# A hybrid encoder on one core: smaller first pieces, a 32-column level, narrow idle products

## The chip, the cores and the metric

The kernel runs on one core of one Trainium2 chip. The metric is the device time of one execution in microseconds. TensorE (PE) multiplies matrices, VectorE (DVE), ScalarE (ACT) and GpSimd (POOL) do the elementwise work, and SyncE (SP) issues most DMA transfers. Every engine works through its own instructions in order.

## The reference, cut to what matters

The input is `x`, 256 tokens by 2048 features, in float32. Two layers follow, and a final RMSNorm. Each layer is RMSNorm, a token mixer, a residual add, RMSNorm, a gated MLP with a depthwise convolution of width 3 (ConvGLU, 5504 hidden features), and a residual add. The mixer of the first layer is a bidirectional mLSTM (8 heads), that of the second a bidirectional HGRN2 (16 heads of 128).

```python
for layer in range(DEPTH):
    hn = rmsnorm(h, norm_mix_g[layer])
    mix = mlstm_mixer(hn, ...) if layer % 2 == 0 else hgrn_mixer(hn, ...)
    h = h + mix
    h = h + conv_glu(rmsnorm(h, norm_ffn_g[layer]), ...)
return rmsnorm(h, final_g)

# HGRN2, one direction: a product of gates f lies between a token t and a source s
lf = log(lb + (1 - lb) * sigmoid(z));  k = (1 - lb) * sigmoid(-z)
attn[t, s] = sum_k q[t, k] * exp(sum of lf over (s, t]) * k[s, k]      # s <= t
o[t] = sum_s attn[t, s] * v[s]                                         # and the same backward in time
```

## The kernel before, in words

**Products and weights.** All weights are read once from memory in float32. ACT rounds each piece to a high part `wh` (line 152), DVE subtracts it from the piece to get the low part `wl` (line 153), and TensorE forms high by high, high by low and low by high. The activations are split in the same way into `xt`: the high half by ACT (line 224), the low half by DVE (line 225). A stream of chunks goes through `stream`, which asks `split_weights` for pieces, three ahead. A piece is loaded by SP into one of three buffers `raw` (line 138, `RAW = 3`); it can be loaded only when DVE has done the last `wl` of the piece that had the buffer. There are four buffers each of `wh` and `wl` (`WB = 4`).

**The first chunk.** It has 16 k-tiles. One k-tile is 128 features: 640 columns of weights (512 for the values of the first heads and 128 for the gates) and 256 columns of `x`. `FIRST` lists the k-tiles at which a piece begins. The x tiles lie in `gx`; tiles 0 and 1 are loaded on ACT's queue (line 143), the later ones by SP, right behind the weights of their piece (line 146). For every k-tile, ACT makes `wh`, DVE makes `wl`, and then `ch.x` splits the x tile; `pin` keeps these in the order in which the program states them. TensorE then makes eight products a tile (lines 213 to 218). At k-tile 10, SP also loads two tables of constants, `cst` and `pp` (line 240). Elsewhere a scheduler orders the instructions of each engine by its own estimate of times, so that an edit in one place can move instructions in another. The chunk after the first is `in_w_aq`, with pieces of 2048 columns (1 MB).

**Idle products.** Before the first chunk TensorE multiplies a tile of ones by itself nine times (line 875). Nothing reads the result. A float32 product is two passes in the records, so this shows as 18.

**HGRN2 heads.** The second layer forms `attn` by levels. At the level of h tokens, pairs of neighbouring blocks of h tokens are joined, for h = 1, 2, 4, ... 64, and 128 by two full products (lines 735 and 736). The operands of levels 1 to 64 are kept as `ms[0]` to `ms[6]`. `product` (line 711) makes eight products, one for each block of 32 source tokens, each of them 32 output partitions high; four neighbours write the four quarters of the partitions. In `pa` (PSUM, 512 columns) lie the full products, level 64 (`ms[6]`) and level 32 (`ms[5]`), both with 64 columns for each block; in `pd` lie the five levels 1 to 16 and the diagonal (`ks`, `q`), with 32 columns for each block. For level 32 the columns are both blocks of the pair, although only the neighbour's block is needed; the other half is overwritten later. ACT copies the diagonal to `AD` (line 742), DVE selects each of the five levels into it under a mask (line 744), ACT copies `pa` to `AT` (line 745) and then puts the four diagonal blocks of `AD` into `AT` (line 748). TensorE multiplies `AT` by the values (`py`, line 759). The generator `head` is advanced by `side.tick` while TensorE runs the chunks, and yields between these stages.

Of the kernel before, what the change touches and what calls it, by code (L numbers as in the profile page):

```python
# [15 lines left out]
P = 128  # L16
T = 256
# [26 lines left out]
WB = 4  # L44
MIX = 5
LEAD = 48
FIRST = (0, 1, 2, 4, 7, 10, 13, 16)

QUAD = 32
LEVELS = (1, 2, 4, 8, 16, 32, 64)  # L50
# [5 lines left out]
def trunk_kernel(ctx, tc, xT, x_d, fg_d, pp_d, cst_d, w_first, w_aq, w_ak, w_av, w_ao, w_aout,  # L56
                 w_bq, w_bv, w_bg, w_bout, w_up, w_down, out, mscr):
    nc = tc.nc
    act, dve, pool, pe = nc.scalar, nc.vector, nc.gpsimd, nc.tensor
# [9 lines left out]
    ones = keep.tile([P, T], F32, name="ones")  # L69
# [12 lines left out]
    def aux(name):  # L82
        return psa.tile([P, 512], F32, tag="aux", name=name)
# [39 lines left out]
    def split_weights(chunks):  # L123

        first = True
        for ch in chunks:
            total = ch.nk * ch.width
            cuts = [0]
            if first:
                cuts = [k * ch.width for k in FIRST]  # L130
            while cuts[-1] < total:
                cuts.append(min(total, cuts[-1] + 2048))
            step = ch.width if first else 1024
            for b0, b1 in zip(cuts, cuts[1:]):
                n = b1 - b0
                raw = wpool.tile([P, 2048], F32, tag="raw", bufs=RAW, name="raw")
                pin = tc.keep_in_program_order if first else lambda ins: ins
                pin(nc.sync.dma_start(raw[:, :n], ch.src[:, b0:b0 + n]))
                if first:
                    k0, k1 = b0 // ch.width, b1 // ch.width  # L140
                    if k0 == 0:
                        for a, b in ((0, KT + T), (KT + T, KT + 2 * T)):
                            nc.scalar.dma_start(gx[:, a:b], xT[:, a:b])
                    elif k0 > 1:
                        a, b = KT + k0 * T, KT + k1 * T
                        pin(nc.sync.dma_start(gx[:, a:b], xT[:, a:b]))
                for c0 in range(0, n, step):
                    m = min(step, n - c0)
                    wh = wpool.tile([P, 1024], F32R, tag="wh", bufs=WB, name="wh")
                    wl = wpool.tile([P, 1024], F32R, tag="wl", bufs=WB, name="wl")  # L150
                    r = raw[:, c0:c0 + m]
                    pin(act.copy(wh[:, :m], r))  # L152
                    pin(dve.tensor_tensor(wl[:, :m], r, wh[:, :m].bitcast(F32), ALU.subtract))  # L153
                    if first:
                        ch.x((b0 + c0) // ch.width, pin)
                    yield wh, wl, m // ch.width
            first = False

    def stream(chunks):
        pieces = split_weights(chunks)  # L160
        ready = []

# [213 lines left out]
    def head_scale(ss, width):  # L376
        rs = ev.tile([P, 2], F32, tag="rs", bufs=6, name="rs")
        dve.tensor_scalar(rs, ss, 1.0 / width, EPS, ALU.mult, ALU.add)
        pool.tensor_tensor(rs, rs, hmx, ALU.pow)
        return rs  # L380
# [242 lines left out]
    def hgrn(norm, nxt):  # L623
# [25 lines left out]
        def blocks(z, h, a, b):  # L649
            v = z[:, 0:2 * (T + h)].rearrange("k (p x) -> k p x", p=2)[:, :, a:b]  # L650
            return v.rearrange("k p (m j) -> k m p j", j=2 * h)[:, :, :, 0:h]

        def gview(g, n, start, h):
            v = g[:, start:start + 2 * (n - 1)].rearrange("k (p x) -> k p x", p=2)[:, :, 0::2]
            return v.rearrange("k p m -> k m p").unsqueeze(3).broadcast_to([P, n // 2, 2, h])
# [28 lines left out]
        def head(hd):  # L684
            mp = box["mp"]
            st = heads[hd]
            while hd and "done" not in heads[hd - 1]:
                yield 0.3
            QZ, KZ = st["QK"][:, 0:640], st["QK"][:, 512:1152]
            q, ks, G = st["q"], st["ks"], st["G"]  # L690
            AT = mp.tile([P, 4, P], F32, tag="AT", bufs=2, name="AT")
            AD = mp.tile([P, 2, QUAD], F32, tag="AD", bufs=2, name="AD")

            def gather(h):

                i = box["turn"] % (4 + MIX)
                box["turn"] += 1
                if i < 4:
                    m = keep.tile([P, 2, T], F32, tag=f"yt{KT - 4 + i}", name=f"kq{i}")
                else:  # L700
                    m = mp.tile([P, 2, T], F32, tag="kq", bufs=MIX, name="kq")
                for j, z in enumerate((KZ, QZ)):
                    dve.tensor_copy(m[:, j].rearrange("k (m p j) -> k m p j", p=2, j=h), blocks(z, h, 0, T))  # L703
                return m[:, 0], m[:, 1]

            def product(pd, k, q, n, at):

                for b in range(8):
                    o, c, t = b % 4 * QUAD, b // 4 * pd.shape[1] // 2, at(b)
                    c += t % P if pd.shape[1] == T else 0  # L710
                    pe.matmul(pd[o:o + QUAD, c:c + n], k[:, b * QUAD:(b + 1) * QUAD], q[:, t:t + n], start=True, stop=True)  # L711

            def both(ps):
                return ps.rearrange("p (a b) -> p a b", a=2)

            step = SPREAD if hd < BH - 2 else STEP
            mask = [cst[:, C_LV + i * QUAD:C_LV + (i + 1) * QUAD].bitcast(I32).unsqueeze(1).broadcast_to([P, 2, QUAD])
                    for i in range(FINE)]
            ms, n = [gather(1)], T
            yield step  # L720
            for li, h in enumerate(LEVELS):
                qa, ka = blocks(QZ, h, 0, T), blocks(KZ, h, 0, T)
                dve.tensor_tensor(ka, ka, gview(G, n, 1, h), ALU.mult)
                dve.tensor_tensor(qa, qa, gview(G, n, n + 1, h), ALU.mult)
                if h < 64:
                    ms.append(gather(2 * h))
                    n //= 2
                    G2 = mp.tile([P, 3 * n], F32, tag=f"G{h}", bufs=2, name="G2")
                    pool.tensor_tensor(G2, G[:, 0:6 * n:2], G[:, 1:6 * n:2], ALU.mult)  # L729
                    G = G2  # L730
                else:
                    st["done"] = True
                yield step
            pa, pd = aux("pa"), aux("pd")
            pe.matmul(pa[:, 2 * P:3 * P], KZ[:, 0:P], QZ[:, T + P:2 * T], start=True, stop=True)
            pe.matmul(pa[:, 3 * P:4 * P], KZ[:, T + P:2 * T], QZ[:, 0:P], start=True, stop=True)  # L736
            product(pa[:, 0:T], *ms[6], 64, lambda b: (b // 2 ^ 1) * 64)
            product(pa[:, 0:T], *ms[5], 64, lambda b: b // 2 * 64)
            for i in reversed(range(FINE)):
                product(pd[:, (i + 1) * 64:(i + 2) * 64], *ms[i], QUAD, lambda b: b * QUAD)  # L740
            product(pd[:, 0:64], ks, q, QUAD, lambda b: b * QUAD)
            act.copy(AD, both(pd[:, 0:64]))
            for i in range(FINE):
                dve.copy_predicated(AD, mask[i], both(pd[:, (i + 1) * 64:(i + 2) * 64]))
            act.copy(AT, pa.rearrange("p (a b) -> p a b", a=4))
            for j in range(4):
                o = slice(j * QUAD, (j + 1) * QUAD)
                act.copy(AT[o, 0:2, o], AD[o])
            yield
            while "V" not in st["qd"]:  # L750
                yield
            V, j = st["qd"]["V"], hd % 4
            py = aux("py")
            y = mp.tile([P, T], F32, tag="y", bufs=4, name="y")
            ss = mp.tile([P, 2], F32, tag="ss", bufs=2, name="ss")
            for t in range(2):
                c = slice(t * P, (t + 1) * P)
                for s in range(2):
                    pe.matmul(py[:, c], AT[:, s if s == t else 2 + s], V[:, s, j * P:(j + 1) * P], start=(s == 0), stop=(s == 1))  # L759
            act.copy(y, py[:, 0:T])  # L760
            for t in range(2):
                jk = ev.tile([P, 512], F32, tag="jk", bufs=1, name="jk")
                act.activation(jk[:, 0:P], y[:, t * P:(t + 1) * P], AF.Square, accum_out=ss[:, t:t + 1])
            st["y"] = (y, head_scale(ss, 128))
# [106 lines left out]
    pool.memset(pad, 0.0)  # L871
    pool.memset(pad[:, 0:4:2], 1.0)
    idle = aux("idle")
    for _ in range(9):
        pe.matmul(idle[:, 0:P], ones[:, 0:P], ones[:, 0:P], start=True, stop=True)
    n0, n1, n2, n3 = Norm("mix_g", 0), Norm("ffn_g", 0), Norm("mix_g", KT), Norm("ffn_g", KT)
    nf = FinalNorm()
    chunks = mlstm(n0, n1)
# [3 lines left out]
    b = c[0].before  # L882
# [92 lines left out]
```

## Time and profile before

| what | value |
|---|---|
| median of 3 runs | 2423.3 us |
| lowest and highest run | 2422.76 and 2424.72 us |
| the profiled execution, its own time | 2424.19 us |
| its span, first to last instruction | 2422.4 us |
| its mean granted clock of TensorE | 0.998 |
| DMA, mean over the span | 187 GB/s |

A row of a group of instructions gives line, engine, operation, the tiles written and read, and a count; then the busy time in us, the mean of one in ns, and the idle time of the engine just before them with what ended it. A row of the timeline gives start, length, engine, line, operation and count. A row of a window gives its length, then for each engine its busy time and instructions, the granted clock of TensorE, the busy share of the DMA engines and GB/s. A row of waits gives who waited for whom, the us in total, the number and the longest.

### The profile page before, as it was taken

The numbers are of one execution on the slowest core, as the hardware profiler recorded it, in microseconds if no ns is written. First come the engines' busy times: TensorE is split into PE (matmuls) and PEld (weight loads), VectorE is DVE, ScalarE is ACT, GpSimd is POOL, SyncE is SP. The second block draws the span as 40 slices with busy tenths as digits, with TensorE's granted clock in tenths as the row PEclk, the third lists the DMA queues.
The fourth block names the chain that finished last, engine by engine and source line by source line (L and its number), as shares of the span: only waits on it lengthen the run. The fifth ranks groups of instructions, "written<-read, shape, count | busy, mean of one in ns | idle before, by whom it ended". The sixth has DMA issues, their size and how long they took to land.

```text
span 2422.4 us, 36761 instructions
## 1 busy us (share of the span) xinstructions
PE 2408.2 (99%) x14586; PEld 2063.2 (85%) x14586; DVE 1695.6 (70%) x2784; ACT 1211.5 (50%) x1831; POOL 161.7 (7%) x223
## 2 busy tenths in 40 slices
PE   9999999999999999999999999999999999999998
PEld 7888888888888888888888888888888888888887
DVE  7766656777645777657888888885777754677754
ACT  6655455444434444445555555545544443444443
POOL 0100000000000000001222222220000000000000
PEclk9999999999999999999999999999999999999999
DMA  8654555555555555555545554555555555555553
GB/s 296 194 181 168 180 180 185 191 191 191 183 195 197 191 191 189 184 192 184 171 162 173 175 175 163 171 180 194 183 190 190 191 186 196 194 190 192 191 190 141
DMA packets 66061, 451.90 MB, mean 187 GB/s; under 512 B 7504, under 2 KB 8016, under 8 KB 13280
## 3 DMA queue, kind: packets, MB, share of 16 engines
q1 hardware_dynamic: 63792, 442.92, 53.8%
q0 software_dynamic: 1232, 5.31, 0.9%
q8 instruction: 114, 1.87, 0.3%
q10 hardware_dynamic: 864, 1.32, 0.2%
q14 instruction: 59, 0.48, 0.1%
HBM read 447.35 MB, written 2.16 MB: 186 GB/s over the span
## 4 chain that ended last, share of the span: by engine, by line
PE 99%; DMA 0%; issue 0%; ACT 0%; DVE 0%; POOLq 0%; POOL 0%; SPq 0%
PE mm L200 36%; PE mm L204 18%; PE mm L213 14%; PE mm L214 13%; PE mm L215 13%; PE pn L531 1%; PE py L759 1%; PE pd L711 1%; PE pz L286 0%; PE pa L711 0%; DMA gx<-in_xT 0%; PE S L517 0%; PE pz L780 0%; DMA raw<-in_w_first 0%; PE pa L736 0%
## 5 line engine op out<-in xcount | busy, mean ns | idle before, releaser
L153 DVE TENSOR_TENSOR wl<-raw,wh 128x1024 fp32r<-128x1024 f32 (+1 forms) x848 | 1032.9, 1219 | 588.5 <-ACT wh L152 580.2
L152 ACT CAST wh<-raw 128x1024 fp32r<-128x1024 f32 (+1 forms) x848 | 881.5, 1041 | 870.8 <-PE mm L215 403.0
L200 PE MATMUL mm<-xt,wh 128*128 128x512 f32 x3776 | 1315.3, 394 | 0.0
L204 PE MATMUL mm<-xt,wl 128*128 128x256 f32 x3776 | 1049.4, 279 | 0.5 <-issue 0.5
L200 PEld LDWEIGHTS mm<-xt,wh 128*128 128x128 f32 x3776 | 707.0, 188 | 161.1 <-issue 0.4
L204 PEld LDWEIGHTS mm<-xt,wl 128*128 128x128 f32 x3776 | 709.9, 188 | 3.2
L215 PE MATMUL mm<-wh,g 128*128 128x512 f32 x674 | 262.8, 390 | 0.0
L213 PE MATMUL mm<-wh,g 128*128 128x512 f32 x674 | 262.5, 389 | 0.0
L214 PE MATMUL mm<-wl,g 128*128 128x512 f32 x674 | 262.3, 389 | 0.0
L213 PE MATMUL mm<-wh,xt 128*128 128x512 f32 x512 | 198.7, 393 | 2.5 <-ACT xt L224 2.5
L214 PE MATMUL mm<-wl,xt 128*128 128x512 f32 x512 | 198.1, 392 | 0.0
L215 PE MATMUL mm<-wh,xt 128*128 128x512 f32 x512 | 197.8, 391 | 0.0
L229 ACT COPY b<-mm 128x256 f32<-128x256 f32 x237 | 87.7, 370 | 174.3 <-PE mm L204 171.8
L213 PEld LDWEIGHTS mm<-wh,g 128*128 128x128 f32 x674 | 126.5, 188 | 26.4
L215 PEld LDWEIGHTS mm<-wh,g 128*128 128x128 f32 x674 | 126.5, 188 | 26.3
L214 PEld LDWEIGHTS mm<-wl,g 128*128 128x128 f32 x674 | 126.5, 188 | 26.0
L213 PEld LDWEIGHTS mm<-wh,xt 128*128 128x128 f32 x512 | 95.3, 188 | 21.8 <-ACT xt L224 3.0
L215 PEld LDWEIGHTS mm<-wh,xt 128*128 128x128 f32 x512 | 96.4, 188 | 19.8
L214 PEld LDWEIGHTS mm<-wl,xt 128*128 128x128 f32 x512 | 96.4, 188 | 19.2 <-DVE wl L153 0.2
L230 DVE TENSOR_TENSOR a<-mm,b 128x256 f32<-128x256 f32 x86 | 36.5, 425 | 52.6 <-ACT b L229 52.6
L703 DVE COPY kq<-QK 128x256 f32<-128x256 f32 x224 | 70.5, 337 | 0.0
L729 POOL TENSOR_TENSOR G<-G 128x384 f32<-128x384 f32 (+2 forms) x96 | 67.8, 706 | 6.3
(206 smaller groups left out, 1833.8 us busy)
## 6 DMA issues: line engine op xcount, KB each, us to landing
raw<-in_w_up SPq DMA_DIRECT2D x172, 1024.0 KB, 4.9
raw<-in_w_down SPq DMA_DIRECT2D x80, 1024.0 KB, 4.8
raw<-in_w_bq SPq DMA_DIRECT2D x48, 1024.0 KB, 5.1
raw<-in_w_ao SPq DMA_DIRECT2D x16, 1024.0 KB, 4.8
raw<-in_w_aout SPq DMA_DIRECT2D x16, 1024.0 KB, 4.8
raw<-in_w_bv SPq DMA_DIRECT2D x16, 1024.0 KB, 4.7
raw<-in_w_bg SPq DMA_DIRECT2D x16, 1024.0 KB, 4.7
raw<-in_w_bout SPq DMA_DIRECT2D x16, 1024.0 KB, 4.8
```

Source lines behind the costliest of these rows:

```text
L152: pin(act.copy(wh[:, :m], r))
L153: pin(dve.tensor_tensor(wl[:, :m], r, wh[:, :m].bitcast(F32), ALU.subtract))
L200: pe.matmul(ps[f], wh[:, c:c + P], x, start=k + kk == 0, stop=False)
L204: pe.matmul(ps[f][:, 0:T], wl[:, c:c + P], x[:, 0:T], start=False, stop=k + kk == ch.nk - 1)
L213: pe.matmul(ps[t], xh, wh[:, c], start=st, stop=False)
L214: pe.matmul(ps[t], xh, wl[:, c], start=False, stop=False)
L215: pe.matmul(ps[t], xl, wh[:, c], start=False, stop=sp)
L229: act.copy(b, ps[:, T:2 * T])
L230: dve.tensor_tensor(dst, ps[:, 0:T], b, ALU.add)
L531: pe.matmul(pn[:, 0:258], w, v, start=(i == 0), stop=(i == len(parts) - 1))
L703: dve.tensor_copy(m[:, j].rearrange("k (m p j) -> k m p j", p=2, j=h), blocks(z, h, 0, T))
L729: pool.tensor_tensor(G2, G[:, 0:6 * n:2], G[:, 1:6 * n:2], ALU.mult)
```

## The change

There are three edits. `FIRST` begins pieces at more k-tiles, so that the pieces of the first chunk are 1, 1, 1, 1, 2, 2, 2, 2, 2 and 2 tiles instead of 1, 1, 2, 3, 3, 3 and 3; and the split of x tile 0 is put ahead of the split of the first weights, on ACT and on DVE. The level of 32 tokens makes only the neighbour's 32 columns of each block; the diagonal product goes to the place in `pa` that this leaves free, `pd` keeps the five fine levels, and ACT copies the diagonal from `pa` in four copies of 32 partitions instead of one from `pd`. The nine idle products of 128 by 128 become 39 of 32 by 120, which go in turn to the four quarters of the partitions.

```diff
-FIRST = (0, 1, 2, 4, 7, 10, 13, 16)
+FIRST = (0, 1, 2, 3, 4, 6, 8, 10, 12, 14, 16)
...
                     r = raw[:, c0:c0 + m]
+                    if first and b0 == 0:
+                        ch.x(0, pin)
                     pin(act.copy(wh[:, :m], r))
                     pin(dve.tensor_tensor(wl[:, :m], r, wh[:, :m].bitcast(F32), ALU.subtract))
-                    if first:
+                    if first and b0:
                         ch.x((b0 + c0) // ch.width, pin)
...
             product(pa[:, 0:T], *ms[6], 64, lambda b: (b // 2 ^ 1) * 64)
-            product(pa[:, 0:T], *ms[5], 64, lambda b: b // 2 * 64)
+            product(pa[:, 0:T], *ms[5], QUAD, lambda b: (b ^ 1) * QUAD)
+            product(pa[:, 0:T], ks, q, QUAD, lambda b: b * QUAD)
             for i in reversed(range(FINE)):
-                product(pd[:, (i + 1) * 64:(i + 2) * 64], *ms[i], QUAD, lambda b: b * QUAD)
-            product(pd[:, 0:64], ks, q, QUAD, lambda b: b * QUAD)
-            act.copy(AD, both(pd[:, 0:64]))
+                product(pd[:, i * 64:(i + 1) * 64], *ms[i], QUAD, lambda b: b * QUAD)
+            for j in range(4):
+                o = slice(j * QUAD, (j + 1) * QUAD)
+                act.copy(AD[o], both(pa[o, 0:T])[:, :, o])
             for i in range(FINE):
-                dve.copy_predicated(AD, mask[i], both(pd[:, (i + 1) * 64:(i + 2) * 64]))
+                dve.copy_predicated(AD, mask[i], both(pd[:, i * 64:(i + 1) * 64]))
             act.copy(AT, pa.rearrange("p (a b) -> p a b", a=4))
...
-    for _ in range(9):
-        pe.matmul(idle[:, 0:P], ones[:, 0:P], ones[:, 0:P], start=True, stop=True)
+    for i in range(39):
+        o = i % 4 * QUAD
+        pe.matmul(idle[o:o + QUAD, 0:120], ones[:, 0:QUAD], ones[:, 0:120], start=True, stop=True)
```

## The prediction, made before the changed kernel had run

> **What bounds the kernel now.** I read the page's busy rows and chain first, then what TensorE waited for, then the first 40 us by stretches.
>
> ```profile
> PE 2408.2 (99%) x14586; PEld 2063.2 (85%) x14586; DVE 1695.6 (70%) x2784; ACT 1211.5 (50%) x1831; POOL 161.7 (7%) x223
> PE 99%; DMA 0%; issue 0%; ACT 0%; DVE 0%; POOLq 0%; POOL 0%; SPq 0%
> PE mm L213 <- ACT xt L224: 2.5, 2, 1.9
> PE pd L711 <- issue: 1.2, 2, 0.6
> PE idle L875 <- POOL ones L869: 1.1, 1, 1.1
> PE mm L204 <- issue: 0.5, 1, 0.5
> ```
>
> TensorE is busy for 2408.2 us of 2422.4 and all its waits sum to 5.3 us, so an edit pays in one of two ways only: it shortens TensorE work, or it removes one of these waits. Busy is not full speed, though; the windows of the first chunk (busy time by engine, then granted clock, DMA share, GB/s) show a second loss:
>
> ```profile
> 5.56:12.74 7.18, 7.18 (x32) 5.64 (x32) 4.37 (x8) 3.33 (x7) 0.00 (x0) 1.00 0.97 341
> 12.74:14.68 1.94, 0.00 (x0) 0.00 (x0) 0.84 (x2) 1.26 (x3) 0.00 (x0) 1.00 0.98 377
> 14.68:18.12 3.44, 3.44 (x9) 2.76 (x10) 2.56 (x5) 3.44 (x6) 0.00 (x0) 0.52 1.02 421
> 18.12:37.08 18.96, 18.96 (x89) 15.67 (x88) 17.63 (x26) 14.17 (x23) 1.24 (x2) 1.00 0.94 352
> ```
>
> The last row is 11 of the 16 k-tiles: 18.96/11 = 1.72 us each. The first chunk, 5.56 to 37.08, takes 31.52 us; 16 tiles at 1.725 need 27.6. The lost 3.9 us are the 1.94 us wait and tile 4 at clock 0.52 (3.44 instead of 1.72). That is all that the start-up edits can win after 5.56. Why tile 4 waited is in the start of the timeline and in the DMA issues (size, us from issue to landing; the DMA rows are in the order of issue: 0.73, 0.73, 5.98, 6.35, 7.42, 10.29, 21.52):
>
> ```profile
> 1.09 3.94 PE L875 MATMUL idle<-ones 128*128 128x128 f32 x18 [1.09 <-POOL ones L869]
> 4.37 0.72 ACT L152 CAST wh<-raw 128x640 fp32r<-128x640 f32 x1 [1.44 <-DMA raw<-in_w_first]
> 5.00 0.50 ACT L224 ACTIVATE xt<-gx 128x256 fp32r<-128x256 f32 x1
> 5.13 0.83 DVE L153 TENSOR_TENSOR wl<-raw,wh 128x640 fp32r<-128x640 f32 x1 [5.13 <-ACT wh L152]
> 5.56 0.73 PE L213 MATMUL mm<-wh,xt 128*128 128x512 f32 x2 [0.53 <-ACT xt L224]
> 5.98 0.33 SPq L138 DMA_DIRECT2D raw<-in_w_first  x1
> 7.42 0.33 SPq L138 DMA_DIRECT2D raw<-in_w_first  x1
> 14.12 0.51 ACT L224 ACTIVATE xt<-gx 128x256 fp32r<-128x256 f32 x1 [0.68 <-DMA gx<-in_xT]
> ...
> raw<-in_w_first SPq DMA_DIRECT2D x1, 320.0 KB, 3.6
> gx<-in_xT ACTq DMA_DIRECT2D x1, 136.0 KB, 3.8
> raw<-in_w_first SPq DMA_DIRECT2D x1, 960.0 KB, 6.6
> gx<-in_xT SPq DMA_DIRECT2D x1, 384.0 KB, 7.7
> raw<-in_w_first SPq DMA_DIRECT2D x1, 960.0 KB, 9.0
> raw<-in_w_first SPq DMA_DIRECT2D x1, 960.0 KB, 9.4
> raw<-in_w_aq SPq DMA_DIRECT2D x1, 1024.0 KB, 9.7
> ```
>
> The weights of tiles 4 to 6 go out at 5.98, when DVE has freed the first raw buffer; their x tiles, 384 KB, sit behind the 960 KB and land at 14.10. ACT's copy starts at 14.12 and TensorE at 14.68. From 16.4 (7.42 + 9.0) to 19.7 (10.29 + 9.4) the queue landed 960 + 384 KB: 407 KB per us. A first transfer of 320 KB took 3.6 us, of which 0.8 are bytes, so 2.8 are fixed.
>
> **Part 1, x tile 0 ahead of the weights.** The step moves two instructions: ACT's xt copy and DVE's subtraction. The x tile lands at 0.73 + 3.8 = 4.53, later than the weights (4.33). ACT therefore waits for x with the weights already there; xt takes 0.50, and wh is queued behind it. In the rows a copy starts 0.09 before the end of the one ahead (5.00 against 4.37 + 0.72), so wh runs from about 4.97 to 5.7, and TensorE, 0.06 later as before (5.50 to 5.56), starts near 5.77: +0.2. DVE does xt's low half under ACT's wh, and wl ends near 6.6 instead of 5.96. In the changed order TensorE does three products first (0.7 us), so it waits 0.15 more. Bounds: a gain of 0.1 if x lands first, a loss of 0.6 (the whole delay of wl). I take +0.35. The first raw buffer comes free near 6.6, not 5.98, and SP's next weights, and the x tile queued behind them, wait for it.
>
> **Part 2, smaller pieces.** Pieces become 1,1,1,1,2,2,2,2,2,2 tiles, in three buffers.
> - Tile 3 now goes out at 6.6 instead of in the first burst. 320 KB land at 10.2, its 128 KB of x 0.3 later; with xt (0.55) it is ready at 11.05, while TensorE ends tile 2 near 11.1. Wait 0 to 0.5; I take 0.2.
> - Tiles 4 and 5 go out at 7.42. 640 + 256 KB behind tile 3 take 2.2 us: 12.7, and ready at 13.25, against TensorE at 13.0: wait 0.25. But the landing at 14.10 was late: 5.98 + 2.8 + 1344/407 is 12.1, so 2.0 us more were lost. How such a lag shrinks with rows two thirds as wide and less queued behind them, no row shows; bounds 0 and 2.0. I take 0.4, near the low end, since the first burst with its short rows shows none: wait 0.65.
> - Tiles 6 and 7 land 2.2 us later, near 15.3, needed at 17.1; tiles 8 and 9 go out when tile 3's buffer is free (11.8), land near 17.5, needed at 20.6. Later ones have more slack.
> Waits of 0.85 take the place of 1.94 us and of tile 4's slow clock (1.72): 3.66 - 0.85 = -2.8. SP issues three more loads of weights and four more of x, at about 0.33 us each by the row of 5.98; cst and pp, the constants, stand behind tile 11's x as they stood behind tile 12's. SP waits for buffers anyway, so I count nothing.
>
> What covers the next chunk: its first 1 MB went out at 21.52 and landed 9.7 later, 5.9 us ahead of its use at 37.08. Now it waits for tile 11's buffer, goes out near 24.5, and the use comes at 34.4. At 6 to 8 us it lands by 32.5, and a cast of 1.6 times the 640 columns of a tile takes 1.1: about 0.8 us of cover. In the changed order ACT also casts four pieces of that chunk, not two, ahead of the copy that starts the gates; nothing of the gates is due in that chunk. I count nothing; with the cover gone it would cost up to 1.5.
>
> **Part 3, level of 32 tokens, and the diagonal in pa.** TensorE's timeline of one head, one line's busy time by form, and the tightest of 16 heads:
>
> ```profile
> 1164.65 0.65 PE L711 MATMUL pa<-kq 128*32 128x64 f32 x32
> 1165.12 0.87 PE L711 MATMUL pd<-kq 128*32 128x32 f32 x78
> 1166.09 0.50 PE L213 MATMUL mm<-wh,xt 128*128 128x512 f32 x1
> ...
> L759 PE MATMUL py<-V,AT 128*128 128x128 f32 x128 | 17.5, 274 | 0.0
> L748 ACT COPY AT<-AD 32x64 f32<-32x64 f32 x64 | 15.5, 243 | 20.4 <-DVE AD L744 19.8
> L742 ACT COPY AD<-pd 128x64 f32<-128x64 f32 x16 | 3.4, 213 | 5.4 <-PE pd L711 5.4
> 1482.80 1.01 ACT L748 COPY AT<-AD 32x64 f32<-32x64 f32 x4 [2.58 <-DVE AD L744]
> 1484.37 0.83 PE L759 MATMUL py<-V,AT 128*128 128x128 f32 x6
> ```
>
> 32 passes of 64 columns take 1165.12 - 1164.65 = 0.47 us, 14.7 ns each; the 96 of 32 columns that follow (8 blocks, 6 products, 2 passes) take 0.97, 10.1 ns each. The change turns 16 passes of the first kind into the second: 16 x 4.6 ns = 0.074 us per head, 1.2 us for 16 heads, all on the path, since nothing there waits. Bounds: 0 and 1.2. ACT gets four copies of about 0.24 for one of 0.213, +0.8 us per head. In the changed order they stand ahead of AT's copy and read pa, which is done before pd, so DVE's selects, queued behind them, start no later. If they do, the tightest head has 1484.37 - 1483.81 = 0.56 us of cover, and loses at most 0.25. I take nothing.
>
> **Part 4, idle products.** 18 wide passes took 3.94 us, 0.219 each. The narrow ones write 32 columns of the array, four neighbours in turn, as the products above do. 14.7 ns x 120/64 = 28 ns at full clock, twice that at half (the 0.52 row took twice as long): 78 x 55 ns = 4.3 us, ending at 5.4, before tile 0 at 5.77. Cost nothing; the cover is 0.4 us.
>
> **Sum**, against the profiled execution (2424.19; span 2422.4 and 1.8 around it): +0.35 - 2.8 - 1.2 = -3.65, so 2420.5. That execution lay 0.9 above the median of 2423.3: I predict 2419.6.
>
> **Rivals.**
> A: the lag of 2 us returns whole, at tile 3 or 4. Then tile 4 is ready at 15.25 against 13.0, a wait of 2.2, and with it comes the clock of 0.52 for one tile, 1.7; with the 0.35 of part 1 that is 4.3 against the 3.66 lost before: the chunk ends 0.6 later, less 1.2 of part 3: 2422.7. For it: the same queue, and a 640 KB piece is no first transfer. Against: less is queued behind it. The Trainium skill, "DMA: Bandwidth & Descriptors", section Measured, tells to batch transfers to 1 MiB or more for three quarters of peak; that speaks against smaller pieces, and by it A would be the likeliest case. The trace agrees for lone transfers (320 KB in 3.6 us, 960 KB in 6.6) but not for queued ones (1344 KB in 3.3). From rows: a buffer's turn is landing plus 2.6 us of casts, three buffers give 6 tiles a turn, and TensorE needs 6 x 1.725 = 10.35, so it decides from a landing of 7.75 us on.
> B: the clock falls at the waits of 0.2 to 0.65 us too. One tile at 0.52 costs 1.7: 2421.3. The Trainium skill, "TensorE: Matmul & The Clock Gate", section Why this matters, puts the limit at idle gaps over about 3 us; by it B has no chance. The trace disagrees: 1.94 us of waiting brought the row of 0.52. What less does, no row shows, so B keeps a chance.
> C, slower: the narrow products don't overlap and the clock stays low. 78 x 0.219 x 120/128 = 16.0 us, ending at 17.1; then all 16 tiles are due and take 27.6: the chunk ends at 44.7, 7.6 later than before, less 1.2: 2429.7. It decides from an end of the idle products past 37.08 + 1.2 - 27.6 = 10.7. Against: pd's 10.1 ns a pass show the overlap; for it: they ran at full clock behind dense work.
> D: no new waits, and the two gaps of 0.6 ("issue") at pd, which depend on where the instruction stream stands, go too: -0.85 - 1.2 more: 2417.5.
>
> **How the numbers follow.** Forecast 0.57, A 0.18, B 0.12, C 0.05, D 0.08. The forecast's own bounds: 0.45 less at the start and no new waits, 0.85, give 2418.3; 0.25 more at the start and part 3 worth nothing give 2421.1. The range 2417.2 to 2423.2 leaves out C and the tails. 0.2% is 4.8 us, about what a measurement of this kernel can tell from no change; that line lies at 2418.5. Under it are D and, as its low end just reaches there, the lowest part of the forecast (0.16 of 0.57, a little over a quarter, since the three runs differ by 2 us): faster 0.24. Slower is C and a little of A with lost cover: 0.06. The rest, 0.70, is within.
>
> **What would show it.** Right: TensorE's first real product near 5.8; waits in the first chunk of under 1 us and no stretch near 0.5 after 6 us; the first chunk over at about 34.4; 32-column passes of pa at about 10 ns; py never waiting. Wrong: tile 3 or 4 ready later than 14; idle products ending after 6; TensorE waiting for the next chunk's wh; heads in which DVE waits longer for AD.

## The result, and the profile after

The changed kernel takes 2419.86 us (median of 20 runs, 2418.93 to 2422.02), the kernel before 2423.59 us beside it. The ratio is 0.9984, with a 95% interval of 0.9978 to 0.9991: 3.7 us less. The forecast was 2419.6. The interval lies below 1, so the gain is clear of the noise, though it stays inside the 0.2% that the prediction drew as its line. So the time came out as predicted, and that was luck: the experiments show that the sum had two wrong terms that cancel, a gain of 2.45 us that did not come and one of 2.2 us that the sum did not hold. One of the executions behind the experiments' table (of e12) took 6219 us; it is left out of that kernel's ratio and moves its median by 0.03 us.

The profiled execution of the changed kernel took 2421.37 us, 1.5 above its median (that of the kernel before lay 0.9 above its own). Its span, busy rows and chain on the page, and then what TensorE waited for:

```profile
span 2419.6 us, 36956 instructions
PE 2406.7 (99%) x14646; PEld 2060.3 (85%) x14646; DVE 1694.1 (70%) x2784; ACT 1221.1 (50%) x1879; POOL 161.7 (7%) x223
PE 98%; DMA 1%; DVE 0%; issue 0%; ACT 0%; SPq 0%; POOLq 0%; POOL 0%; DVEq 0%
```

```profile
PE mm L215 <- ACT xt L226: 2.1, 3, 0.8
PE idle L880 <- POOL ones L873: 1.1, 1, 1.1
PE mm L215 <- ACT wh L154: 0.8, 1, 0.8
PE mm L216 <- DVE wl L155: 0.2, 1, 0.2
```

The waits for x tiles did not go: there are three now instead of one long one. What went are the rows with "issue", which is idle time for which the profile shows nothing that TensorE waited for: 1.2 us at `pd` and 0.5 in the products of another chunk.

The timeline of the start (TensorE, ACT, SP and GpSimd), and the first row of the next chunk:

```profile
1.09 3.77 PE L880 MATMUL idle<-ones 128*32 128x120 f32 x78 [1.09 <-POOL ones L873]
4.49 0.51 ACT L226 ACTIVATE xt<-gx 128x256 fp32r<-128x256 f32 x1 [1.56 <-DMA gx<-in_xT]
5.67 0.73 PE L215 MATMUL mm<-wh,xt 128*128 128x512 f32 x2 [0.80 <-ACT wh L154]
6.50 0.33 SPq L138 DMA_DIRECT2D raw<-in_w_first  x1
11.44 0.51 ACT L226 ACTIVATE xt<-gx 128x256 fp32r<-128x256 f32 x1 [1.03 <-DMA gx<-in_xT]
12.00 0.50 PE L215 MATMUL mm<-wh,xt 128*128 128x512 f32 x1 [0.71 <-ACT xt L226]
14.58 0.49 PE L215 MATMUL mm<-wh,xt 128*128 128x512 f32 x1 [0.53 <-ACT xt L226]
29.91 0.73 PE L215 MATMUL mm<-wh,xt 128*128 128x512 f32 x2 [0.85 <-ACT xt L226]
32.86 0.73 PE L216 MATMUL mm<-wl,xt 128*128 128x512 f32 x2 [0.23 <-DVE wl L155]
37.73 0.40 PE L202 MATMUL mm<-xt,wh 128*128 128x512 f32 x1
```

The idle products end at 4.86 and delay nothing. Tile 3 waits 0.71 us, tile 4 0.53, tile 12 0.85; behind the last of these waits tiles 12 and 13 take 1.98 and 2.35 us instead of 1.73. The first chunk is over at 37.73, 0.65 later than in the profile before. What comes ahead of the first two waits (windows: granted clock, DMA share and GB/s last), first of the kernel before, then of the changed one:

```profile
6.00:7.00 1.00, 1.00 (x6) 0.86 (x5) 0.78 (x2) 0.95 (x2) 0.00 (x0) 1.00 0.97 391
7.00:8.00 1.00, 1.00 (x6) 0.82 (x6) 0.79 (x2) 0.46 (x1) 0.00 (x0) 1.00 0.94 212
```

```profile
6.00:7.00 1.00, 1.00 (x5) 0.62 (x4) 1.00 (x2) 1.00 (x3) 0.00 (x0) 1.00 0.11 36
7.00:8.00 1.00, 1.00 (x7) 0.83 (x6) 1.00 (x3) 0.68 (x2) 0.00 (x0) 1.00 0.58 74
8.00:14.00 6.00, 5.29 (x24) 3.81 (x22) 2.05 (x4) 1.93 (x3) 0.00 (x0) 1.00 0.94 322
```

With three pieces of one tile the first burst is nearly over at 6 us, and the next piece, which waits for a buffer, goes out at 6.50. In two microseconds 110 KB move instead of 603, roughly 490 KB that come later: 1.2 us of the queue's 407 KB per us. x tile 3 lands at 11.4 and those of tiles 4 and 5 at 14.0. In all eight profiles with the smaller pieces, those of the experiments included, the queue is thin from 6 to 8 us (104 to 300 KB), and the x tiles of 4 and 5 land at 13.5 to 14.2.

The heads of the second layer, here the fourth of 16: three rows of the kernel before, with the gap inside its narrow products, and then the changed kernel:

```profile
1244.82 0.65 PE L711 MATMUL pa<-kq 128*32 128x64 f32 x32
1246.84 0.27 PE L711 MATMUL pd<-q,ks 128*32 128x32 f32 x8 [0.58 <-issue]
1247.04 0.50 PE L200 MATMUL mm<-xt,wh 128*128 128x512 f32 x1
```

```profile
1245.50 0.56 PE L713 MATMUL pa<-kq 128*32 128x64 f32 x32
1245.87 0.33 PE L713 MATMUL pa<-q,ks 128*32 128x32 f32 x14
1246.05 0.87 PE L713 MATMUL pd<-kq 128*32 128x32 f32 x78
1246.85 0.39 PE L206 MATMUL mm<-xt,wl 128*128 128x256 f32 x1
```

From the first narrow product to the next wide one this head took 2.22 us before and takes 1.35 now. In the kernel before 12 heads took about 1.44, three (the 4th, 8th and 12th) 2.22, 2.25 and 2.00, and the 16th, whose block comes in two parts, 1.73; all 16 together took 25.53 us. In the changed kernel 15 take 1.34 to 1.38 and the 16th 1.59, together 21.91. These sums are of rounded rows, good to about 0.05 us. Of the 3.62 us, 16 x 0.09 = 1.44 are the narrower products and 2.18 are the three gaps.

### The profile page after: what moved, and what is told of

Its sections match the earlier page's. It is cut to its first block, busy times and chain, and to the rows that moved or that the text cites. A ratio compares the mean times of both kernels' runs of the same rounds, so it can differ in the third digit from the quotient of the medians.

```text
span 2419.6 us, 36956 instructions
## 1 busy us (share of the span) xinstructions
PE 2406.7 (99%) x14646; PEld 2060.3 (85%) x14646; DVE 1694.1 (70%) x2784; ACT 1221.1 (50%) x1879; POOL 161.7 (7%) x223
## 4 chain that ended last, share of the span: by engine, by line
PE 98%; DMA 1%; DVE 0%; issue 0%; ACT 0%; SPq 0%; POOLq 0%; POOL 0%; DVEq 0%
PE mm L202 36%; PE mm L206 18%; PE mm L215 13%; PE mm L216 13%; PE mm L217 13%; DMA gx<-in_xT 1%; PE pn L533 1%; PE py L763 1%; PE pd L713 0%; PE pz L288 0%; PE pa L713 0%; PE S L519 0%; PE pz L784 0%; PE pa L738 0%; PE pa L737 0%
```

## The experiments

The table gives, for every kernel, the profiled execution's end of the first chunk, the sum of its 16 narrow blocks of the heads, and the median with its ratio and interval against the kernel before measured beside it (2423.05, 2423.31 and 2423.26 us in the three groups).

| kernel | first chunk over | blocks | median us | ratio |
|---|---|---|---|---|
| before | 37.08 | 25.53 | | |
| head edit alone (e1) | 34.94 | 23.97 | 2422.29 | 0.9996 [0.9987, 1.0005] |
| narrow idle products alone (e2) | 36.37 | 23.35 | 2420.92 | 0.9991 [0.9982, 0.9999] |
| first-chunk edits alone (e3) | 39.46 | 24.70 | 2425.72 | 1.0011 [1.0002, 1.0019] |
| smaller pieces alone (e4) | 35.26 | 24.80 | 2423.79 | 1.0002 [0.9993, 1.0011] |
| 60 passes more, wide idle kept (e8) | 34.76 | 23.37 | 2420.60 | 0.9992 [0.9983, 1.0001] |
| head and idle, first chunk as before (e9) | 35.96 | 21.91 | 2419.66 | 0.9985 [0.9977, 0.9994] |
| changed kernel again (e10) | 36.02 | 21.89 | 2419.38 | 0.9984 [0.9975, 0.9993] |
| x loads moved in the program only (e6) | 37.69 | 21.83 | 2421.00 | 0.9988 [0.9979, 0.9996] |
| x loads held back (e11) | 35.69 | 21.87 | 2419.47 | 0.9984 [0.9975, 0.9992] |
| as e11, x tile 0 behind the weights (e12) | 35.42 | 21.91 | 2418.82 | 0.9982 [0.9973, 0.9991] |
| as e9, x loads held back (e13) | 36.02 | 21.86 | 2421.26 | 0.9989 [0.9980, 0.9997] |
| as e3, x loads held back (e14) | 36.47 | 25.15 | 2423.12 | 0.9999 [0.9990, 1.0007] |

### The three edits apart

Head edit alone (e1): only `product` on `ms[5]`, the diagonal in `pa` and the four copies.

> The kernel before with the head edit alone (level of 32 tokens in 32-column products, the diagonal in pa, four small copies to AD). Theory one (the prediction's split): 16 passes a head fall from 14.7 to about 10 ns, so the narrow block of a head takes 0.07 to 0.09 us less, 1.2 to 1.4 us in all, time ratio about 0.9995; the three heads of the kernel before with a gap of 0.6 to 0.8 us in their narrow block keep it. Theory two (the head edit also removes those gaps, because it moves the instructions): the sixteen narrow blocks together go from 25.5 to about 22 us, -3.5, ratio about 0.9985. Both: the first chunk still ends near 37.1 us.

The blocks went to 23.97: theory one for the head, 1.34 to 1.38 us in 12 blocks, and the same three heads keep gaps (2.13, 2.00 and 2.03). Theory two falls: the head edit does not take the gaps away. The expectation's common part failed in a telling way. The code of the start is that of the kernel before, yet the first chunk ended at 34.94, 2.1 us earlier: tile 4 waited 1.13 us instead of 1.94 and the clock stayed up. One profile's first chunk is not the kernel's.

Narrow idle products alone (e2):

```diff
-    for _ in range(9):
-        pe.matmul(idle[:, 0:P], ones[:, 0:P], ones[:, 0:P], ...)
+    for i in range(39):
+        o = i % 4 * QUAD
+        pe.matmul(idle[o:o + QUAD, 0:120], ones[:, 0:QUAD], ones[:, 0:120], ...)
```

> The kernel before with the 78 narrow idle passes alone. Theory one (they overlap and only warm the clock): they end before 5.4 us, the first chunk ends within 0.2 us of 37.1, the heads' narrow blocks keep 25.5 us, time ratio 1.0000 within 0.0003. Theory two (the gaps in the heads depend on where the instruction stream stands, and 60 more instructions at the start move it): the gaps move to other heads or vanish, the blocks' sum changes by 0.5 to 2 us either way although no head is edited, ratio 0.9991 to 1.0008. If the idle passes also keep the clock up, the stretch at clock 0.52 near 15 us is gone, and the first chunk ends 1.7 us earlier, near 35.4.

Theory two, a little beyond its 2 us. No head was edited, and the blocks fell by 2.18 us because all three gaps went; the median fell by 2.1. The clock stayed up, but tile 4 waited 2.40 us, so the first chunk ended at 36.37 and not near 35.4. Its waits hold no "issue" row:

```profile
PE mm L213 <- ACT xt L224: 2.9, 2, 2.4
PE idle L876 <- POOL ones L869: 1.1, 1, 1.1
```

First-chunk edits alone (e3):

> The kernel before with both edits of the first chunk (smaller pieces, x tile 0 ahead of the weights), wide idle products and heads as before. The prediction's split: waits of 0.85 us in place of 1.94 and no clock of 0.52, first chunk over at about 34.4 us, time 2.4 us less, ratio 0.9990. Theory two (read from the changed kernel's trace): the early waits shrink to 0.7 + 0.5 us, but later tiles (12 and 13) wait about 1.1 us, because their transfers meet the GpSimd queue's 1 MB of x; with the restart after every wait the first chunk ends at 37 to 38 us, no gain, ratio 0.9997 to 1.0003.

Worse than either theory: tile 12 waited 2.46 us, the clock fell behind it, and the chunk ended at 39.46. The timeline at tile 12, and the window behind it (granted clock, DMA share, GB/s last):

```profile
30.86 1.04 PE L215 MATMUL mm<-wh,xt 128*128 128x512 f32 x2 [2.46 <-ACT xt L226]
```

```profile
30.86:34.05 3.19, 3.19 (x9) 2.53 (x10) 2.73 (x4) 3.19 (x6) 0.00 (x0) 0.54 0.17 72
```

Smaller pieces alone (e4), `FIRST` only:

> The kernel before with the smaller pieces alone; x tile 0 stays behind the weights. The prediction's working: the start stays at 5.56, the first buffer is free at 6.0, tile 3 lands 0.6 us earlier than with x ahead, so the first chunk ends 0.35 us or more before the one of both edits: near 34.0, ratio 0.9988. Theory two: tile 3 waits less (0.1 to 0.7 us), but tiles 12 and 13 wait as in the changed kernel, first chunk over at 36.8 to 37.5, ratio 0.9996 to 1.0002.

Tile 3 did not wait; tile 4 waited 1.61 us, and there was no wait at tile 12. The chunk ended at 35.26, but this execution was the fastest of its kernel's runs (2422.60 against a median of 2423.79), and the median shows no gain. Between the two theories; it does not decide.

### Why the gaps went

e8 keeps the nine wide idle products and the heads of before and adds only this:

```diff
+    for _ in range(30):
+        pe.matmul(idle[0:QUAD, 0:8], ones[:, 0:QUAD], ones[:, 0:8], start=True, stop=True)
```

> The kernel before with its nine wide idle products and 30 more of 8 columns behind them, so 60 passes more ahead of tile 0, as many as the narrow ones add; nothing else. Theory one (the gaps in the heads vanished because the instruction stream behind the idle products stands 60 passes further on): no 'issue' gap at pd, the sixteen narrow blocks sum to 23.3 us instead of 25.5, time 2.2 us less, ratio 0.9991. Theory two (narrow products of 120 columns at the start did it in another way, by the clock or by the array's columns): the blocks keep two or three gaps, 24.7 to 25.5 us, ratio 0.9997 to 1.0003.

Theory one: blocks 23.37, no gap, median 2.7 us less, with an interval that just includes 1. So what counts for the gaps is not the form of the idle products but how many instructions stand ahead of the heads; only one number, 60 passes more, was tried. The trace shows what the instruction stream is cut into (DMA queues of the kernel before: of the whole span, then of the stretch around the fourth head, 1243.32 to 1246.02; in e2 no such row stands around that head):

```profile
q8 instruction: 114, 1.87, 0.3%
```

```profile
q8 instruction: 1, 0.02, 2.9%
```

114 packets of 16.4 KB for 2 x 14586 matmul and load instructions are 256 instructions a packet, as many as the 128 passes of a head's block have with their loads. A block uses a packet's worth in 1.44 us. The trace has the start of every packet. Those that lie from 1.5 us ahead of a block's start to 1.4 behind it are these, against that start, in us, with the head's number:

```
before   gaps at heads 4, 8, 12: -0.57 -0.49 -0.31    no gap: +0.41 (1) +1.07 (5) +1.14 (13)
e1       gaps at heads 4, 8, 12: -0.35 -0.46 -0.28    no gap: +0.26 (1) +1.00 (5) +1.01 (9)
e3       gaps at heads 4, 8:     -0.20 -0.56          no gap: -0.30 (12) +0.61 (1) +1.36 (5) +1.11 (13)
e4       gaps at heads 4, 8:     -0.36 -0.53          no gap: -0.31 (12) +0.61 (1) +1.09 (5)
e14      gaps at heads 4, 8:     -0.53 -0.43          no gap: +0.13 (12) +0.29 (1) +1.09 (5) +1.22 (13)
the nine profiles with 60 passes more, no gap: 42 packets, all at -1.16 or earlier or at +0.95 or later
```

Every gap has a packet 0.2 to 0.6 us ahead of its block, and of 14 packets in that stretch two (head 12 of e3 and of e4) came without a gap. 60 passes more are 120 instructions, 0.47 of a packet, which moves all 16 heads out of that stretch. That the instructions run out there is inferred from this; no row records it. The Trainium skill, "Runtime: NRT & Kernel Launch", section Instruction fetch mechanics, says that instructions are refilled in blocks of 16 KiB, 256 instructions, and that crossing a boundary is mostly hidden. The trace agrees on the block (16.4 KB, 256); where a crossing is not hidden, in dense narrow products, it cost 0.56 to 0.81 us in the kernel before and up to 1.08 in e14.

### What the first-chunk edits are worth

e9 is the changed kernel with the first chunk of before:

> The changed kernel with its first chunk as before: the head edit and the narrow idle products alone. Theory one (the start-up edits gain nothing or lose): the blocks of the heads sum to 21.9 us as in the changed kernel, first chunk over at 35 to 37 us with one wait of 1 to 2.4 us at tile 4; time 3.6 us under the kernel before or more, ratio 0.9975 to 0.9986, so no slower than the changed kernel. The prediction's split (start-up -2.45): ratio 0.9994, 2.4 us slower than the changed kernel.

2419.66: theory one. The blocks' 3.62 us are the whole gain, and the first-chunk edits are worth nothing that these runs can tell (0.9985 with them taken out, 0.9984 with them).

e10 is the changed kernel once more:

> The changed kernel again, a second look at its start. If the landing of the first loads differs from execution to execution, tiles 3, 4 and 12 wait by other amounts than 0.7, 0.5 and 0.85 us, and the first chunk ends between 34.5 and 39 us, while the heads' blocks keep 21.9 us to 0.1. If the start is the same in every execution, it ends within 0.3 us of 37.7. Ratio 0.9984 either way, as measured before.

The start differs: tile 3 waited 1.00 us, tiles 4 and 12 not at all, and the chunk was over at 36.02 instead of 37.73. The wait at tile 12 is thus not in every execution.

e6 moved GpSimd's loads of `x` from `done_first` to `done_o` in the program:

> The changed kernel with GpSimd's two loads of x (1 MB each, into hm, needed by the first residual only) issued at the first head's end instead of in the first chunk. Theory one (these 2 MB take the DMA engines from tiles 12 to 15): the transfers issued near 19 us land in 6 to 7 us instead of 9.8, tile 12 does not wait, no wait after tile 4, first chunk over at 35.5 to 36.3 us, 1.5 to 2 us less than in the changed kernel, ratio to the kernel before 0.9976 to 0.9979. Theory two (the queue of the weights is slow by itself): tile 12 still waits 0.5 us or more, ratio 0.9984 as the changed kernel.

Inconclusive: the load still went out where it was (21.88 in the changed kernel, 21.86 here), and tile 12 waited 0.95 us. That the scheduler left it there because nothing that it depends on had changed is likely, but was not tried. e11 gives the load something to wait for:

```diff
                 for t in range(2):
+                    pool.tensor_copy(hm[:, t, 0:1], norm.rc[:, t:t + 1])
                     pool.dma_start(hm[:, t], x_d[t])
```

> The changed kernel with GpSimd's two loads of x held back: before each, GpSimd copies one column of the norm's factor rc into the target, and rc exists only after the first chunk (42.4 us in the changed kernel); the loads overwrite the column. Theory one (GpSimd's first megabyte takes three quarters of the DMA engines from 26 to 29 us, and the x tiles of 12 to 15 that have not landed by then wait for it): tile 12 never waits, the transfers issued near 19.5 land in 6 to 7.5 us, only the waits at tiles 3 and 4 stay (about 1 us together); the first chunk ends at 35 to 36.1, and the runs differ less; median 0.5 to 1.5 us under the changed kernel, ratio to the kernel before 0.9978 to 0.9982. Theory two (the weights' own queue is late): tile 12 waits in some executions as before, ratio 0.9984. If the two loads now meet the weights of the chunks behind 43 us, TensorE waits for wh there, 1 us or more.

Tile 12 does not wait. The queues from 26 to 29 us (q1 carries weights and x tiles, q0 GpSimd's load; packets, MB, share of the 16 engines), first in the changed kernel, then in e11, and then GpSimd's timeline in the same order:

```profile
q0 software_dynamic: 124, 0.95, 74.8%
q1 hardware_dynamic: 129, 0.34, 28.4%
```

```profile
q1 hardware_dynamic: 251, 1.21, 101.3%
```

```profile
21.88 0.70 POOL L602 DMA_DIRECT2D gx<-in_x  x1 [20.11 <-DMA pp<-in_pp]
```

```profile
41.06 1.25 POOL L603 DMA_DIRECT2D gx<-in_x  x2 [0.46 <-DMA raw<-in_w_ak]
```

In those 3 us GpSimd's megabyte takes three quarters of the engines. Nearly as many packets went through from each queue, 124 and 129, but GpSimd's are of 7.7 KB and the others of 2.6. The x tiles of 12 and 13, issued at 19.51, then took 9.8 us and landed at 29.33; in e10, where they took 6.3 and landed at 26.00, they were through just as it began. In e11 they took 6.8. No wait for `wh` came up behind 41 us. The median is that of the changed kernel and not 0.5 to 1.5 less; only the spread shrank, 2419.07 to 2420.12 against 2418.77 to 2421.21 in e10. So theory one's mechanism is supported: with the load in place three of the five profiles with the smaller pieces wait for x at tile 12 (the changed kernel, e3, e6), and with it held back none of three (e11, e12, e14). The price that it put on it is not seen in the median.

e14 does the same to e3:

> The kernel before with the smaller pieces, x tile 0 ahead and the loads of x held back; wide idle products, heads as before. The same two start-up edits without the hold were 2.7 us slower than the kernel before (1.0011). Theory one (they lost it to GpSimd's load at tile 12): no wait at tile 12, first chunk over by 36.5, time 1 to 2 us under the kernel before, ratio 0.9992 to 0.9997. Rival (they lost it to cold or dropped clock that the wide idle products leave, or to their own queue): still 1.0005 or more.

No x tile waited at 12, and the chunk was over at 36.47 instead of 39.46; the median is 2.6 us under that of e3, whose interval lay above 1. The ratio itself, 0.9999, lies between theory one's 0.9992 to 0.9997 and the rival's 1.0005: the blocks took 25.15 us and tile 4 waited 1.49. That the collision made e3 slower than the kernel before is supported; that nothing else did is not.

e12 takes the x tile ahead out again, e13 the smaller pieces too:

> As the run with the loads of x held back, but x tile 0 behind the weights as in the kernel before. The prediction's working for x ahead (+0.35): TensorE starts at 5.5 instead of 5.7, tile 3's weights go out at 6.0 instead of 6.5, tile 3 waits 0 to 0.2 us instead of 0.5 to 1.0; first chunk over at 34.5 to 35.3, 0.4 to 0.8 us less than with x ahead. Rival (the order is of no account, since tile 4 then waits for what tile 3 no longer does): within 0.3 us of it.

> Head edit, narrow idle products and the loads of x held back; the first chunk in its old pieces of 1, 1, 2, 3, 3, 3, 3 tiles. If the smaller pieces are worth something once nothing meets them, this one keeps the wait of 1 to 2.4 us at tile 4 and ends the first chunk 0.5 to 1.5 us later than the smaller pieces do, at 35.5 to 36.4. If not, both end together within 0.3 us, and the smaller pieces bring nothing here.

e12 is the fastest kernel of all: 2418.82, ratio 0.9982, 0.65 us under e11 in the median, 0.27 in the end of the first chunk (35.42). The sign of the prediction's part 1 holds. Its size stays open: the 0.65 of the medians fits the working, the 0.27 of the profiles the rival, for tile 3 no longer waits 0.29 us and tile 4 waits 0.85 in both. The intervals of e12 and of the changed kernel overlap. e13 keeps its wait of 1.85 us at tile 4, ends the chunk 0.6 later than e12 (36.02), and its median is 2.4 higher. With GpSimd's load in place the smaller pieces were worth nothing that these runs can tell (e9 against e10).

Part of that 2.4, and how e13 came out 1.6 above e9, which differs only in the load, is in the mean granted clock of the single executions. It is 0.998 in the two profiled ones that have a stretch at half clock (before and e3) and 0.999 in the twelve that have none. Five of e13's eleven executions have 0.998 and took 2421.26 to 2422.10 us, one of e9's has it (2421.34); the others have medians of 2419.79 and 2419.58, so little of the 1.6 is left. e12 has none, and against e13's executions at 0.999 it is 1.0 us faster: about that is what the smaller pieces are worth here at the same recorded clock.

## Why the prediction was right, and where it was not

**Part 1, +0.35.** Not contradicted: TensorE started at 5.67 (5.77 foreseen), the buffer was free for SP at 6.50 (6.6), and tile 0 took 2.00 us instead of 1.83; together +0.28. e12 against e11 gives +0.27 to +0.65. One pair of profiles does not resolve the start, though: with x tile 0 ahead it lay at 5.51 to 5.82 in six profiles, with it behind at 5.44 to 5.80 in seven (e8 left out, where the idle products last longer).

**Part 2, -2.8.** Wrong, and the largest error. The term that failed is the lag of 0.4 at tiles 4 and 5, "near the low end": their x tiles landed at 14.0 and not at 13.1. Against the 12.7 of the working without a lag that is 1.3 us, and 0.8 to 1.45 in the eight profiles with the smaller pieces. x tile 3 came at 11.4 instead of 10.5, but within 0.4 us of its weights, as foreseen, in five of those eight. The weights of tile 3 came even earlier than foreseen (9.7 against 10.2), so the thin queue from 6 to 8 us was no more than the fixed 2.8 us of the working. What the working did not hold is in the window behind it: from 8 to 14 us the queue moved 322 KB per us and not 407, 1930 KB in all, while tiles 3 to 5 needed 1344. The piece of tiles 6 and 7, issued at 8.37, moved at the same time; that this is what held up the x tiles fits the numbers, but was not tried. It also priced a wait at its own length: tile 3 took 2.06 us after its wait and tile 4 2.15, against 1.73; that the casts are then only just ahead is likely, but was not tried. At the end of tile 4 (16.7) the forecast, 34.4 less 11 tiles, stood at 15.4. And "Later ones have more slack" failed at tile 12: GpSimd's load is in none of the prediction's steps. Lastly, the 3.66 us that were to be won were those of one execution; the same code in e1 lost about 1.7 (34.94 - 5.66 - 27.6). Of the 101 executions of the kernel before beside the experiments only 21 have the mean clock of 0.998, so the 1.72 us of tile 4's slow clock were in the profile, but not in the median.

**Cover of the next chunk.** In the changed kernel no wait for its `wh` shows. In e3 the cover was gone, 1.1 us for its `wl`, inside the 1.5 that was given.

**Part 3, -1.2.** Right, and a little low: 1.44 to 1.35 us a head, 1.44 in all. The four copies and the selects cost nothing, as said (groups of the changed kernel, then a row of its waits on DVE):

```profile
L746 ACT COPY AD<-pa 32x64 f32<-32x64 f32 x64 | 13.0, 203 | 11.9 <-PE pa L713 11.0
L763 PE MATMUL py<-V,AT 128*128 128x128 f32 x128 | 17.5, 274 | 0.0
```

```profile
DVE AD L748 <- ACT AD L746: 4.3, 4, 1.1
```

Four copies of 203 ns instead of one of 213 are +0.6 us of ACT a head (0.8 foreseen); `py` never waits; DVE waits for `AD` 4.3 us in all, against 6.7 before.

**Part 4, nothing.** The end came at 4.86, ahead of the foreseen 5.4, but "cost nothing" was wrong: the 60 passes more brought 2.18 us in the heads, a millisecond later. The prediction had the two gaps and their dependence on the place of the stream in rival D, at 1.2 us and with a chance of 0.08, and did not ask which edit moves the stream, though this one plainly adds 60 passes ahead of it.

**Rivals.** A came in part: 1.3 of the lag's 2 us came back, without the slow clock. B fell: no wait of 0.2 to 1.0 us in the changed kernel brought the clock down. C fell: the idle passes overlap even at the start, 78 in 3.77 us. Of D the gaps came true, three and not two, and the missing waits not. The sum of what happened, -1.44 - 2.18 and nothing from the start, is -3.6; the sum of the prediction was -3.65: that the two agree is luck.

## What to carry to other kernels

Before pricing a stall at the start of a kernel, see whether a second execution of the same code has it; a loss of 3.9 us in one profile was 1.7 in another. Smaller first pieces shorten the burst that fills the queue: count the bytes that do not move, those of later pieces that move at the same time, the transfers of other queues that the moved ones now meet, and the slow tile behind each wait. And where a profile shows "issue" gaps in dense runs of short instructions, adding or removing instructions far ahead can end or make them, so an edit's time can have nothing to do with what it edits.

## What had not been expected of the hardware

Sixty passes more ahead of the first chunk, in either of two shapes, took three gaps of 0.56 to 0.81 us out of heads more than a millisecond later. GpSimd's 1 MB load, once it ran, had 75% of the DMA engines and left 28% to the queue of the weights. Starting late cost nothing where arrival was the limit: with the 60 extra passes of e8 the first product came at 6.87 us instead of 5.56, its list of waits has no tile of the first chunk, and the chunk ended at 34.76, the earliest of all. The slow clock behind a wait is not a matter of the wait's length alone: with the wide idle products it came after 1.94 us (0.52, before) and 2.46 us (0.54, e3) and not after 1.61 (e4), 1.49 (e14) or 1.13 (e1); with the narrow ones it did not come after 2.40 (e2), 2.02 (e9) or 1.85 (e13). The Trainium skill, "TensorE: Matmul & The Clock Gate", section Why this matters, puts the limit at gaps over about 3 us; the first two rows lie under it. What the traces do show is when the clock changes. In their clock records every stretch between two changes is a whole number of 3.413 us: 3, 1 and 703 in the kernel before, 7, 1 and 699 in e3, 705 to 707 in the others. The windows of the slow stretch and the one ahead of it, of the kernel before and then of e3 (granted clock third from the end; the slow stretch is set at its bounds here, so 0.50 stands for the 0.52 and 0.54 of the wider windows):

```profile
4.61:14.85 10.24, 7.77 (x37) 6.04 (x36) 5.81 (x10) 5.66 (x11) 0.00 (x0) 1.00 0.98 352
14.85:18.26 3.41, 3.41 (x9) 2.73 (x10) 2.52 (x5) 3.41 (x7) 0.00 (x0) 0.50 1.01 419
```

```profile
7.20:31.08 23.88, 20.80 (x95) 16.63 (x94) 14.65 (x25) 14.01 (x25) 0.70 (x1) 1.00 0.98 355
31.09:34.50 3.41, 3.41 (x10) 2.66 (x10) 2.95 (x5) 3.41 (x7) 0.00 (x0) 0.50 0.12 50
```

Counted in such periods, the 1.94 us of the kernel before lie whole in the period that ends at 14.85, and the 2.46 of e3 in the one that ends at 31.09. The 2.40 of e2 are cut by the end of a period (14.76) into 1.68 and 0.72, the 2.02 of e9 (14.20) into 1.15 and 0.87, the 1.85 of e13 (14.38) into 1.10 and 0.75; the other waits are shorter than 1.68 altogether. So all eight fit a limit between 1.68 and 1.94 us of idling within one period, with wide and narrow products alike, and a protection by the narrow ones is not needed to explain them. This is inferred: no run moved a wait across the end of a period and left the rest alone. The periods do not start with the program: in four executions with the same start (the changed kernel, e10, e11, e6) the first record of full clock begins at 4.27, 4.63, 4.84 and 5.82 us. By this a wait of about 2 us brings the slow clock in some executions and not in others.
